# Five table stores of a two-block transformer kernel, issued from GpSimd's queue instead of SyncE's

## The chip, the cores and the metric

The kernel runs on one core of one Trainium2 chip. The metric is the device time of one execution in microseconds (us), lower is better. A core has five engines with an instruction queue each: TensorE (PE, matrix products), VectorE (DVE), ScalarE (ACT), GpSimd (POOL) and SyncE (SP, which here only issues DMA transfers). Any of SP, ACT and POOL can issue a DMA; the transfers themselves run on 16 DMA engines.

## The reference

Two transformer blocks run one after the other on a sequence of T = 512 rows of width D = 1024, all in float32. The first block mixes with an mLSTM and a stick-breaking attention and ends with an MLP; the second is a sparse attention with three branches (compressed, selected, window), each with a relative position bias. The two places that matter here:

```python
def first_block(...):
    ...
    x = x + y.astype(x.dtype) @ w_out[l]
    h2 = rms_norm(x, norm_mlp_g[l])
    x = x + jnp.square(jax.nn.relu(h2 @ w_up[l])) @ w_down[l]      # the MLP, d_ff = 4096
    return x

def nsa_compressed(q, kc, vc, table):                              # second block
    ...
    bias = table[t5_bucket(dist)].astype(jnp.float32)              # table: 32 buckets x 16 heads
    p = masked_softmax(logits + bias, dist >= 0)
```

The bias depends on the distance and the head alone, so it can be made long before the attention that uses it.

## The kernel before, in words

**Weights.** All weight matrices lie in DRAM as a list of tiles of 128 x 1024 float32 (512 KB), in the order of use. The class Weights walks through it. For each tile, SP loads it into a buffer wr (L169; three buffers), ACT casts it to a rounded high part wh (L172; four buffers), and DVE or POOL takes the difference as a low part wl (L174; four buffers). A product is then three matmuls: high x high, high x low, low x high (L341 to L343 in `gen_t`, L374 to L376 in `gen_n`).

**The MLP** (`mlp`, L740) runs in two halves f. In each, 16 steps m = 0 to 15 make 128 hidden columns each: `proj_t` does 24 matmuls with one weight tile into one PSUM bank b, and then ACT reads the bank with Relu (L761), squares (L763) and rounds it (hh, L305), and DVE takes the low part hl. Then `proj_n` multiplies by the second matrix. The eight PSUM banks are used in a ring.

**The tables.** In half 0, ahead of step m = 6, `bias_tables` makes two tables for the second block. The first, tr, has 16 rows (one a head) of 384 floats. It is stored to the DRAM tensor bt_d, repeated 128 times for each head, in four DMAs of 16 x 32 x 384 floats (768 KB each). The second, cb, is the compressed branch's table, stored to cb_d in one DMA of 128 x 2048 floats (1024 KB). The second block reads bt_d at L1256 and cb_d at L1031.

**What sets the order.** Each engine works through its own list in order, and the lists are fixed when the program is built. In the MLP a scheduler sets them from an estimate of its own of when things are ready; it is not the order of the Python lines. In the second block PE and POOL follow the written order. Before the change the five stores are handed to SP one at a time, ahead of steps m = 7 to 11 (`stores.pop(0)()`, L757).

Of the kernel before, what the change touches and what calls it, by code (L numbers as in the profile page):

```python
# [253 lines left out]
def tile_blocks(ctx, tc, x, xt, wts, prm, cst, table, post_g, w2k, w2v, out):  # L254
    nc = tc.nc
    v, s, g, pe, sy = nc.vector, nc.scalar, nc.gpsimd, nc.tensor, nc.sync
# [6 lines left out]
    def ring(*ids):  # L263
        turn = [0]

        def take():
            i = ids[turn[0] % len(ids)]
            turn[0] += 1
            return banks.tile([128, T], F32, name=f"b{i}", tag=f"b{i}", bufs=1)
        return take  # L270
# [17 lines left out]
    def small(shape, name, bufs=2):  # L288
        return glob.tile(shape, F32, name=name, tag=name, bufs=bufs)

    def ts(out_, in_, s1, s2=None, op0=OP.mult, op1=None, eng=None):
        if s2 is None:
            (eng or v).tensor_scalar(out_, in_, s1, None, op0)
        else:
            (eng or v).tensor_scalar(out_, in_, s1, s2, op0, op1)  # L295

    def stt(out_, a, sc, b, op0, op1):
        v.scalar_tensor_tensor(out_, a, sc, b, op0, op1)  # L298

    def tt(out_, a, b, op=OP.mult, eng=None):  # L300
        (eng or v).tensor_tensor(out_, a, b, op)  # L301

    def hi_lo(hi, lo, src, hi_in=None, scale=None):
        if scale is None:
            s.copy(hi, src)  # L305
            tt(lo, src, hi.bitcast(F32), OP.subtract)
        else:
            s.activation(hi, src, AF.Identity, scale=scale)
            stt(lo, src, scale, hi.bitcast(F32), OP.mult, OP.subtract)
# [39 lines left out]
    def proj_t(psum, acts, w=None, m=128):  # L349
        got = []  # L350
        emit(gen_t(psum, acts, got.append, w, m))
        return got[0]
# [28 lines left out]
    def proj_n(psum, acts, tail=1):  # L381
        got = {}
        emit(gen_n(psum, acts, got.__setitem__, tail))
        return [got[tb] for tb in range(4)]

    def transposed_acts(psum, src, gain):
        acts = []
        for kt in range(KT):
            ps = psum()
            for tb in range(4):  # L390
                pe.transpose(ps[:, 128 * tb:128 * tb + 128], src[:, tb, 128 * kt:128 * kt + 128], ident)
            h, l = act_tiles(kt)
            hi_lo(h, l, ps, scale=col(gain, kt))
            acts.append((h, l))
        return acts
# [294 lines left out]
    bt_d = dram.tile([16, 128, 384], F32, name="bt_d")  # L690
    x2_d = dram.tile([128, 4, D], F32, name="x2_d")
    cb_d = dram.tile([128, 4, 16, 32], F32, name="cb_d")

    def bias_loads(pb):
        tb_ = pb.tile([32, 16], F32, name="tb_")
        sy.dma_start(tb_, table)
        t31 = pb.tile([32, 16], F32, name="t31")
        sy.dma_start(t31, table[31:32, :].to_broadcast([32, 16]))
        oh = pb.tile([32, 384], F32, name="oh")
        sy.dma_start(oh, cst[0:32, C_OH:C_OH + 384])  # L700
        mr = pb.tile([16, 384], F32, name="mr")
        sy.dma_start(mr, cst[0:16, C_MASKR:C_MASKR + 384])
        ohc = pb.tile([128, 512], F32, name="ohc")
        sy.dma_start(ohc, cst[:, C_OHC:C_OHC + 512])
        mc = pb.tile([128, 16], F32, name="mc")
        sy.dma_start(mc, cst[:, C_MASKC:C_MASKC + 16])
        tt(tb_, t31, tb_, OP.subtract)
        bd = pb.tile([128, 4, 16], F32, name="bd")
        v.memset(bd, 0.0)
        for i in range(4):  # L710
            v.tensor_copy(bd[32 * i:32 * i + 32, i, :], tb_)
        return tb_, oh, mr, ohc, mc, bd

    def bias_tables(psum, pb, tb_, oh, mr, ohc, mc, bd):
        ps = psum()
        pe.matmul(ps[0:16, 0:384], tb_, oh, start=True, stop=True)
        tr = pb.tile([16, 384], F32, name="tr")
        tt(tr, ps[0:16, 0:384], mr, OP.add)
        ps = psum()
        for i in range(4):  # L720
            pe.matmul(ps[:, 64 * i:64 * i + 64], ohc[:, 128 * i:128 * i + 128],
                      bd.rearrange("p a b -> p (a b)"), start=True, stop=True)
        near = pb.tile([128, 16, 16], F32, name="near")
        tt(near, ps[:, 0:256].rearrange("p (k h) -> p h k", h=16),
           mc[:, None, :].to_broadcast([128, 16, 16]), OP.add)
        cb = pb.tile([128, 4, 16, 32], F32, name="cb")
        v.memset(cb, -NEG)
        for tb in range(4):
            lo, hi = max(0, 8 * tb - 9), 8 * tb + 7
            if lo > 0:  # L730
                v.memset(cb[:, tb, :, 0:lo], 0.0)
            k0 = lo - 8 * tb + 9
            v.tensor_copy(cb[:, tb, :, lo:hi], near[:, :, k0:k0 + hi - lo])
        stores = [(lambda i: lambda: sy.dma_start(bt_d[:, 32 * i:32 * i + 32, :],
                                                  tr[:, None, :].to_broadcast([16, 32, 384])))(i) for i in range(4)]
        stores.append(lambda: sy.dma_start(cb_d, cb))
        return stores

    def mlp(x1):
        with tc.tile_pool(name="ml", bufs=1) as ml, tc.tile_pool(name="pb", bufs=1) as pb:  # L740
            pj = ring(*range(8))
            acts = transposed_acts(pj, x1, P_GMLP)
            tables = bias_loads(pb)
            ssq2 = small([128, 2, 4], "ssq2", 1)
            ssq = small([128, 4], "ssq")
            for tb in range(4):
                jk = glob.tile([128, D], F32, name="jk2", tag="wr", bufs=3)
                s.activation(jk, x1[:, tb, :], AF.Square, accum_out=ssq[:, tb:tb + 1])
            r2 = small([128, 4], "rs2")
            ts(r2, ssq, 1.0 / D, EPS, OP.mult, OP.add)  # L750
            v.reciprocal(r2, r2)
            for f in range(2):
                hid = []
                for m in range(16):
                    if f == 0 and m == 6:
                        stores = bias_tables(pj, pb, *tables)
                    if f == 0 and m > 6 and stores:  # L757
                        stores.pop(0)()
                    ps = proj_t(pj, acts)
                    a = ml.tile([128, T], F32, name="a", tag="ra", bufs=2)  # L760
                    s.activation(a, ps, AF.Relu)  # L761
                    a2 = ml.tile([128, T], F32, name="a2", tag="ra2", bufs=2)
                    s.activation(a2, a, AF.Square)  # L763
                    h = ml.tile([128, T], F32R, name="hh", tag="hh", bufs=18)
                    l = ml.tile([128, T], F32R, name="hl", tag="hl", bufs=18)
                    hi_lo(h, l, a2)
                    hid.append((h, l))
                for c in range(2):
                    ps = proj_n(pj, hid, 1 + 3 * f * c)
                    for tb in range(4):  # L770
                        xs = x1[:, tb, 512 * c:512 * c + 512]
                        stt(xs, ps[tb], r2[:, tb:tb + 1], xs, OP.mult, OP.add)
                        if f == 1:
                            sy.dma_start(x2_d[:, tb, 512 * c:512 * c + 512], xs)
                            jk = glob.tile([128, T], F32, name="jk4", tag="rb", bufs=1)
                            s.activation(jk, xs, AF.Square, accum_out=ssq2[:, c, tb:tb + 1])

        return ssq2
# [569 lines left out]

    xb = first_mixer()
    sums2 = mlp(xb)  # L1350
    with tc.manual_schedule(engines={mybir.EngineType.PE, mybir.EngineType.Pool}):
        nsa(xb, sums2)
# [55 lines left out]
```

## Time and profile before

| | |
|---|---|
| median of 3 runs | 1399.81 us (1399.77 to 1400.01) |
| the profiled execution | 1398.81 us |
| its span, first to last instruction | 1397.1 us |
| PE busy | 1337.3 us, 96% of the span |
| DVE, ACT, POOL busy | 58%, 47%, 19% of the span |
| mean granted TensorE clock | 0.990 of full speed |
| DMA, mean over the span | 90 GB/s |

The profile is of one execution. PE is busy nearly all the time, so what counts is where it is not, and where it runs at the lower clock. The times of the trace are us from the first instruction.

### The profile page before, as it was taken

What the parts mean: (1) busy time and instruction counts of PE and PEld (TensorE: products, weight loads), DVE (VectorE), ACT (ScalarE), POOL (GpSimd) and SP (SyncE); (2) the same over time, 40 slices, a digit from 0 to 9 for tenths busy, and PEclk for the clock granted to TensorE, in tenths of its full rate; (3) what the DMA queues carried; (4) which work ended last, traced back from release to release, by engine and by line L of the source; (5) the groups of instructions that cost most, each with busy time, mean ns of one, the idle gap of its engine ahead of it and who ended that gap; (6) DMA issues with size and microseconds to landing.
All of it is one profiled execution on the core that took longest, in us unless ns stands there. A gap on an engine that the chain in (4) does not pass through costs nothing.

```text
span 1397.1 us, 17790 instructions
## 1 busy us (share of the span) xinstructions
PE 1337.3 (96%) x6622; PEld 1090.3 (78%) x6622; DVE 808.5 (58%) x1596; ACT 650.6 (47%) x1273; POOL 261.2 (19%) x230
## 2 busy tenths in 40 slices
PE   9999999999999999989999999899788999999897
PEld 7977787778786888868888888788677878777776
DVE  4678535556667535232233323455988998988823
ACT  6577624443434325341135422254446656665522
POOL 0022101111101000000000000134536242333352
PEclk9999999999999999999999999999999999999999
DMA  7411121213131414843333323314223122121132
GB/s 232 137 46 47 61 91 61 91 49 103 46 106 46 154 57 142 110 166 92 100 94 93 104 91 121 125 50 130 75 71 106 54 61 61 53 68 46 55 121 76
DMA packets 42039, 125.31 MB, mean 90 GB/s; under 512 B 4528, under 2 KB 11232, under 8 KB 41696
## 3 DMA queue, kind: packets, MB, share of 16 engines
q1 hardware_dynamic: 41952, 124.17, 29.4%
q8 instruction: 52, 0.85, 0.2%
q14 instruction: 35, 0.29, 0.1%
HBM read 115.77 MB, written 8.39 MB: 89 GB/s over the span
## 4 chain that ended last, share of the span: by engine, by line
PE 59%; DVE 16%; issue 15%; ACT 6%; POOL 2%; DMA 1%; SPq 0%; POOLq 0%; DVEq 0%; ACTq 0%
PE b L375 9%; PE b L374 9%; PE b L376 9%; PE b L341 8%; PE b L343 8%; PE b L342 8%; DVE P L295 4%; DVE b L1176 2%; DVE ptall L301 2%; ACT wh L172 1%; PE b L827 1%; ACT P L1180 1%; PE b L1211 1%; PE b L544 1%; PE b L1195 1%
## 5 line engine op out<-in xcount | busy, mean ns | idle before, releaser
L172 ACT CAST wh<-wr 128x1024 fp32r<-128x1024 f32 (+3 forms) x204 | 207.6, 1020 | 385.9 <-PE b L376 222.7
L341 PE MATMUL b<-ah,wh 128*128 128x512 f32 x808 | 330.5, 409 | 6.3 <-ACT wh L172 5.9
L174 DVE TENSOR_TENSOR wl<-wr,wh 128x1024 fp32r<-128x1024 f32 (+2 forms) x142 | 169.2, 1194 | 281.1 <-ACT wh L172 280.7
L343 PE MATMUL b<-ah,wl 128*128 128x512 f32 x808 | 318.9, 395 | 0.6 <-DVE wl L174 0.5
L342 PE MATMUL b<-al,wh 128*128 128x512 f32 x808 | 318.2, 394 | 0.0
L343 PEld LDWEIGHTS b<-ah,wl 128*128 128x128 f32 x808 | 152.8, 189 | 35.4 <-DVE wl L174 1.8
L341 PEld LDWEIGHTS b<-ah,wh 128*128 128x128 f32 x808 | 153.0, 189 | 34.3 <-ACT wh L172 6.7
L174 POOL TENSOR_TENSOR wl<-wr,wh 128x1024 fp32r<-128x1024 f32 (+1 forms) x62 | 143.6, 2320 | 159.0 <-ACT wh L172 149.4
L342 PEld LDWEIGHTS b<-al,wh 128*128 128x128 f32 x808 | 153.4, 190 | 24.5 <-issue 0.5
L374 PE MATMUL b<-wh,ah 128*128 128x512 f32 (+3 forms) x352 | 125.9, 359 | 1.0 <-ACT wh L172 0.6
L376 PE MATMUL b<-wh,al 128*128 128x512 f32 (+3 forms) x352 | 125.5, 357 | 0.1
L375 PE MATMUL b<-wl,ah 128*128 128x512 f32 (+3 forms) x352 | 125.3, 356 | 0.1
L1180 ACT ACTIVATE P<-b,nm 128x128 f32<-128x128 f32 (+3 forms) x128 | 67.5, 528 | 104.8 <-DVE nm L1176 102.6
L375 PE MATMUL b<-wl,hh 128*128 128x512 f32 x256 | 102.1, 399 | 0.0
L374 PE MATMUL b<-wh,hh 128*128 128x512 f32 x256 | 100.9, 394 | 0.0
L376 PE MATMUL b<-wh,hl 128*128 128x512 f32 x256 | 100.4, 392 | 0.0
L295 DVE TENSOR_SCALAR P<-P,rd,gn 128x128 f32<-128x128 f32 (+3 forms) x128 | 93.4, 730 | 2.5
L301 POOL TENSOR_TENSOR rsr<-rsm,mhalf 128x2 f32<-128x2 f32 (+1 forms) x3 | 2.4, 802 | 476.6 <-DVE rsm L295 476.6
L374 PEld LDWEIGHTS b<-wh,ah 128*128 128x128 f32 x352 | 66.2, 188 | 9.8 <-ACT wh L172 0.9
L376 PEld LDWEIGHTS b<-wh,al 128*128 128x128 f32 x352 | 66.4, 189 | 8.8 <-DVE al L298 0.5
L375 PEld LDWEIGHTS b<-wl,ah 128*128 128x128 f32 x352 | 66.4, 189 | 8.4 <-DVE wl L174 0.5
L1195 PE MATMUL b<-ident,P 128*128 128x128 f32 x320 | 56.7, 275 | 12.7 <-DVE ptall L301 10.4
(286 smaller groups left out, 2213.5 us busy)
## 6 DMA issues: line engine op xcount, KB each, us to landing
wr<-in_wts_dram SPq DMA_DIRECT2D x188, 512.0 KB, 3.5
bt_d<-tr SPq DMA_DIRECT2D x4, 768.0 KB, 20.5
wr<-in_wts_dram SPq DMA_DIRECT2D x8, 280.0 KB, 2.6
xk<-in_xt_dram SPq DMA_DIRECT2D x8, 256.0 KB, 3.8
xn<-in_x_dram SPq DMA_DIRECT2D x4, 512.0 KB, 4.9
xbig<-in_x_dram SPq DMA_DIRECT2D x1, 2048.0 KB, 9.9
x_d<-xbig SPq DMA_DIRECT2D x8, 256.0 KB, 2.9
bt<-bt_d SPq DMA_DIRECT2D x8, 256.0 KB, 2.7
```

Of the source, the lines that this page charges most:

```text
L172: nc.scalar.copy(hi, raw)
L174: eng.tensor_tensor(lo, raw, hi.bitcast(F32), OP.subtract)
L295: (eng or v).tensor_scalar(out_, in_, s1, s2, op0, op1)
L301: (eng or v).tensor_tensor(out_, a, b, op)
L341: pe.matmul(o, a, ah, start=(kt == 0), stop=False)
L342: pe.matmul(o, a, al, start=False, stop=False)
L343: pe.matmul(o, b, ah, start=False, stop=(kt == KT - 1))
L374: pe.matmul(o, ah[:, tsl], a, start=(kk == 0 and k == 0), stop=False)
L375: pe.matmul(o, ah[:, tsl], b, start=False, stop=False)
L376: W.last = pe.matmul(o, al[:, tsl], a, start=False, stop=end)
L1180: latest[0] = s.activation(P[:, 0:n], S[:, 0:n], AF.Exp, bias=nm, scale=-1.0, accum_out=rd)
L1195: pe.transpose(pst[:, 128 * sb:128 * sb + 128], P[:, 128 * sb:128 * sb + 128], ident)
```

## The change

`bias_tables` no longer returns a list of stores for `mlp` to hand out; it issues all five itself, at its end, on POOL's queue (`g` is GpSimd, `sy` is SyncE). What is stored, and where to, is the same.

```diff
-        stores = [(lambda i: lambda: sy.dma_start(bt_d[:, 32 * i:32 * i + 32, :],
-                                                  tr[:, None, :].to_broadcast([16, 32, 384])))(i) for i in range(4)]
-        stores.append(lambda: sy.dma_start(cb_d, cb))
-        return stores
+        for i in range(4):
+            g.dma_start(bt_d[:, 32 * i:32 * i + 32, :], tr[:, None, :].to_broadcast([16, 32, 384]))
+        g.dma_start(cb_d, cb)
...
                 for m in range(16):
                     if f == 0 and m == 6:
-                        stores = bias_tables(pj, pb, *tables)
-                    if f == 0 and m > 6 and stores:
-                        stores.pop(0)()
+                        bias_tables(pj, pb, *tables)
                     ps = proj_t(pj, acts)
```

The lists of instructions change in three places. On SP, in half 0 of the MLP, the stores stood between loads of weight tiles (wr); the difference of the two lists there is:

```order
-L169 DMA wr<-in_wts_dram 128x1024 x9
-L734 DMA bt_d<-tr 16x32x384 x3
-L169 DMA wr<-in_wts_dram 128x1024
-L734 DMA bt_d<-tr 16x32x384
-L169 DMA wr<-in_wts_dram 128x1024
-L736 DMA cb_d<-cb 128x2048
-L169 DMA wr<-in_wts_dram 128x1024 x48
+L169 DMA wr<-in_wts_dram 128x1024 x59
```

The five stores are gone and the loads stand in one row of 59. On POOL they now stand together between the last instruction of the first mixer (L626) and the first of the second block (the second L301 here, a power of -1/2):

```order
 L626 AFFINE_SELECT be<-be 128x128
+L735 DMA bt_d<-tr 16x32x384 x4
+L736 DMA cb_d<-cb 128x2048
 L301 TENSOR_TENSOR rsr<-rsm,mhalf 128x2
```

On ACT, though no line of the diff is about it, the scheduler has put four casts of weight tiles elsewhere. Before, this stood there from the end of step m = 10 to the Relu of step m = 13 (b_5017, b_5056 and b_5095 are the PSUM banks of steps 11, 12 and 13; wh<-wr is the cast of a weight tile for a later step):

```order
L305 CAST hh<-a_5004 128x512
L761 ACTIVATE a<-b_5017 128x512
L763 ACTIVATE a_5044<-a 128x512
L305 CAST hh<-a_5044 128x512
L172 CAST wh<-wr 128x1024
L761 ACTIVATE a<-b_5056 128x512
L763 ACTIVATE a_5083<-a 128x512
L305 CAST hh<-a_5083 128x512
L172 CAST wh<-wr 128x1024 x4
L761 ACTIVATE a<-b_5095 128x512
```

And now, for the same steps:

```order
L305 CAST hh<-a_5005 128x512
L172 CAST wh<-wr 128x1024
L758 ACTIVATE a<-b_5017 128x512
L760 ACTIVATE a_5044<-a 128x512
L305 CAST hh<-a_5044 128x512
L172 CAST wh<-wr 128x1024
L758 ACTIVATE a<-b_5056 128x512
L760 ACTIVATE a_5083<-a 128x512
L305 CAST hh<-a_5083 128x512
L172 CAST wh<-wr 128x1024
L758 ACTIVATE a<-b_5095 128x512
```

Before, no cast stands between the banks of steps 7 and 11; one follows step 11 and four follow step 12. Now one cast stands behind every step. DVE's differences wl move with them in the same way against its hl. Apart from this, the lists of PE, DVE, ACT and POOL hold the same instructions in the same order as before, down to the end of the program.

## Rows read from the trace of the kernel before

**Rows 1.** The page: span, TensorE's busy time, the chain that ended last

```profile
span 1397.1 us, 17790 instructions
...
PE 1337.3 (96%) x6622; PEld 1090.3 (78%) x6622; DVE 808.5 (58%) x1596; ACT 650.6 (47%) x1273; POOL 261.2 (19%) x230
...
PE 59%; DVE 16%; issue 15%; ACT 6%; POOL 2%; DMA 1%; SPq 0%; POOLq 0%; DVEq 0%; ACTq 0%
```

**Rows 2.** Waits, 540 to 640 us: who waited for whom, total us, times, longest

```profile
PE b L341 <- ACT wh L172: 5.9, 2, 2.9
...
ACT wh L172 <- DMA wr<-in_wts_dram: 3.2, 1, 3.2
```

**Rows 3.** PE's timeline in half 0: start us, us, instruction, idle before and releaser

```profile
561.18 0.48 PE L341 MATMUL b<-ah,wh 128*128 128x512 f32 x1
...
593.73 0.39 PE L343 MATMUL b<-ah,wl 128*128 128x512 f32 x1
597.06 0.50 PE L341 MATMUL b<-ah,wh 128*128 128x512 f32 x1 [2.94 <-ACT wh L172]
...
604.56 0.39 PE L343 MATMUL b<-ah,wl 128*128 128x512 f32 x1
607.89 0.73 PE L341 MATMUL b<-ah,wh 128*128 128x512 f32 x1 [2.94 <-ACT wh L172]
...
620.74 0.39 PE L341 MATMUL b<-ah,wh 128*128 128x512 f32 x1
...
626.19 0.39 PE L374 MATMUL b<-wh,hh 128*128 128x512 f32 x1
```

**Rows 4.** ACT's timeline in half 0, columns as in the rows of PE

```profile
559.41 1.04 ACT L172 CAST wh<-wr 128x1024 fp32r<-128x1024 f32 x1 [2.58 <-PE b L342]
...
572.17 1.05 ACT L172 CAST wh<-wr 128x1024 fp32r<-128x1024 f32 x1 [2.58 <-PE b L342]
...
577.84 0.60 ACT L761 ACTIVATE a<-b 128x512 f32<-128x512 f32 x1 [2.81 <-PE b L343]
...
594.15 0.60 ACT L761 ACTIVATE a<-b 128x512 f32<-128x512 f32 x1 [3.53 <-PE b L343]
...
595.97 1.04 ACT L172 CAST wh<-wr 128x1024 fp32r<-128x1024 f32 x1
...
606.79 2.94 ACT L172 CAST wh<-wr 128x1024 fp32r<-128x1024 f32 x3
```

**Rows 5.** Windows of 4 us: length, busy by engine, granted clock, DMA share, GB/s

```profile
556.00:560.00 4.00, 4.00 (x18) 2.73 (x17) 0.97 (x2) 1.39 (x3) 0.00 (x0) 1.00 0.42 135
...
564.00:568.00 4.00, 4.00 (x19) 3.30 (x19) 0.48 (x3) 1.27 (x2) 0.00 (x0) 1.00 0.92 99
...
596.00:600.00 4.00, 2.41 (x6) 1.69 (x7) 1.92 (x2) 1.01 (x2) 0.00 (x0) 0.72 0.90 349
...
604.00:608.00 4.00, 1.05 (x6) 0.56 (x5) 0.82 (x2) 2.96 (x5) 0.00 (x0) 1.00 0.00 0
608.00:612.00 4.00, 3.90 (x10) 2.62 (x11) 3.36 (x3) 1.73 (x2) 0.00 (x0) 0.58 0.43 120
```

**Rows 6.** SP's queue in time: start us, us of issuing, transfers

```profile
560.95 5.10 SPq L734 DMA_DIRECT2D bt_d<-tr  x3
566.17 4.42 SPq L169 DMA_DIRECT2D wr<-in_wts_dram  x1
...
898.84 0.62 SPq L1031 DMA_DIRECT2D Pc<-cb_d  x1
```

**Rows 7.** DMA issues of the whole span: count, KB each, median us to landing

```profile
bt_d<-tr SPq DMA_DIRECT2D x4, 768.0 KB, 20.5
...
cb_d<-cb SPq DMA_DIRECT2D x1, 1024.0 KB, 19.4
```

**Rows 8.** The tile wr, 530 to 640 us: its 19 loads, us to landing

```profile
DMA to landing us min/median/max: 3.3/3.6/21.4
```

**Rows 9.** POOL's timeline around the place of the stores

```profile
883.52 0.69 POOL L301 TENSOR_TENSOR rsr<-rsm,mhalf 128x2 f32<-128x2 f32 x1 [448.67 <-DVE rsm L295]
```

## The prediction

> **What bounds the kernel now.** I read the page first: PE is busy for 1337.3 of 1397.1 us, and the chain that ended last runs mostly over PE [rows 1]. Work that is taken off another engine is therefore worth nothing by itself; the change can only pay where PE stands still or runs at its lower clock. So the second view was the list of waits around the five stores. It has PE waiting twice for a cast of a weight tile, 2.9 us each time, and ACT waiting once for a weight transfer, 3.2 us [rows 2].
>
> Third, PE's timeline gives the price of this stretch. Step m = 6 starts at 561.18, and `proj_n`, which follows step 15, at 626.19 [rows 3]: 65.01 us for ten steps. An undisturbed step, the last of them, takes 626.19 - 620.74 = 5.45 us, so ten should take 54.5. The stretch loses **10.5 us**. Step 11's last matmul starts at 593.73 and, at 0.23 us a matmul (5.45 / 24), is through at 593.96; step 12 starts at 597.06. Step 12 in turn is through at about 604.8 and step 13 starts at 607.89; both gaps are put down to the cast wh [rows 3]. The idle time is 2 x 2.94 = 5.9 us of the 10.5; the rest is the clock, which after the gaps is granted at 0.72 and 0.58 over 4 us where it was 1.00 before them [rows 5], so part of each window runs at 1.2 instead of 2.4 GHz.
>
> Fourth, why the cast is late. Up to step 8 ACT casts one tile a step, as soon as PE gives a buffer free (559.41, 572.17) [rows 4]. Then comes a run of Relu groups with no cast, from 577.84 to the one at 594.15, and the next cast is at 595.97, behind step 11's own Relu group [rows 4]. ACT's list puts it there. Step 12 needs this cast, so PE can't start before ACT has read what PE has just made: the gap is built into the order. It is the same at 606.79, where three casts run in a row behind step 12's group [rows 4]. In that window, 604 to 608 us, the DMA share is 0.00 [rows 5]: no transfer was under way, so the second gap is the order's and not a transfer's. (At the first gap the engines are 0.90 busy [rows 5], so there the trace alone does not separate the two.)
>
> **The change part by part.**
>
> *SP loses five stores.* Three of them hold SP for 5.10 us from 560.95, and the load behind them, step 12's tile, is issued at 566.17 over 4.42 us [rows 6]. PE waits for none of this directly: price 0. But that load can now be issued as soon as its wr buffer is free. There are four wh buffers, so the cast at 559.41, which waits for step 5's last use of one [rows 4], is for step 9; its wr buffer is free once DVE has taken the difference behind it, at about 563 (an estimate: the cast ends at 560.45, and DVE has tr to make first). The load moves some 3 us earlier.
>
> *POOL gains five stores.* POOL's next instruction runs at 883.52 after 448.67 us of idle time [rows 9], and the tables are first read at 898.84 [rows 6]. From 561 on that leaves 322 us. Neither POOL's time to make the transfers nor their landing is on the path unless the whole takes fifteen times the 20.5 us that one store took [rows 7]. Price 0; without that cover it would push the second block's start.
>
> *ACT's and DVE's lists.* One cast stands behind every step, so step 12's tile can be cast at about 577 to 578, when step 8 frees its buffer, instead of 595.97. If its data is there, both gaps go, and with them the time at the lower clock: **minus 10.5 us**. PE's list is the same, and so is everything behind the MLP; the waits of the later stages are between PE, ACT and DVE and don't know at what time they start, so I let the 10.5 us through to the end.
>
> *The transfers themselves.* The same bytes go over the same 16 engines, so this is where the gain could be lost. The stores alone run at 0.92 busy and 99 GB/s [rows 5], and four of 0.786 MB take 3.15 MB / 0.099 = 31.8 us, 29.2 us of busy engines. The weight loads in 556 to 560 move 135 GB/s at a share of 0.42, so 321 GB/s when busy [rows 5]: 1.6 us for a tile of 0.524 MB, every 5.45 us, or 30% of the engines. At that rate cb's 1.05 MB [rows 7] take 3.3 us. Stores are then 32.5 us of work. If the loads get the 30% that they ask for, the stores are done about 32.5 / 0.7 = 46 us after 561, at 607, and no load is short. Before, SP's queue was shared: a load behind stores took up to 21.4 us to land instead of 3.6 [rows 8]. No row shows two queues side by side. Lower bound for a load: 3.6 us. Upper bound: it gets nothing until all stores are through, at 561 + 32.5 = 593.5, and lands at about 597. I take turn and turn about, a load of 4 to 10 us, because a load is asked for 14 us ahead of its cast (three buffers wr, 5.45 us a step, less the difference) and the cast stands another three steps ahead of its use: even 21.4 us would leave PE running.
>
> The Trainium skill, "DMA: Bandwidth & Descriptors", section "Queues, rings and completion order", says that each DMA engine goes round the queues that have work, a packet at a time; by it the loads get their turns, as in the sum. No run here shows it so far.
>
> *A new queue in use.* The execution is 1.7 us longer than its span (1398.81 against 1397.1 [rows 1]). I know of no row for what a first transfer from POOL adds there or at the end; between 0 and another 1.7 us, and I take 0.
>
> *Sum.* 1398.81 - 10.5 = 1388.3 for the profiled execution. That one is 1.0 under the median of the runs, 1399.81, so the median should be **1389.3 us**.
>
> **The rivals.** A difference of 0.2%, 2.8 us, is about what a measurement of this kernel can tell from none.
>
> *B, the loads come last.* POOL's stores are all queued within a short time, and if the engines favour them, step 12's tile lands at the upper bound, 597. The cast adds 1.04 us, so PE stands from 593.96 to 598: 4 us, and some 2 us of lower clock (before, 2.94 us of idle time cost 5.2 in all). Step 13 follows without a gap, since its tile lands 1.6 us later and has a cast of its own. Gain 10.5 - 6 = 4.5: 1395.3 us. For it: the share of 0.92 shows that the stores alone can fill the engines. Against it: nothing in the trace favours one queue.
>
> *C, nothing changes.* The stores are not removed, only issued elsewhere, and the engines stay as full. The Trainium skill, in the same page's section "Issuing engines are not separate DMA queues", says that the issuing engine changes only the sequencer's issue time, usually small beside the transfer. Taken alone, the trace's form of it is that SP's issue time is off the path, price 0, and the time stays at 1399.8 us. Against it stands the DMA share of 0.00 in the second gap: there PE waited for ACT's order, and that does change. What would still give 1399.8 is a first load so late that one stall costs as much as the two, PE starting step 12 at 593.96 + 10.5 = 604.5.
>
> *D, slower: transfers issued by POOL are less efficient.* If the same stores kept the engines busy twice as long and went first, they would be through at 561 + 65 = 626, step 12's tile at about 630 and its cast at 631. PE would stand 37 us: 1399.8 - 10.5 + 37 = 1426 us. It turns into a loss when step 12's cast ends behind 604.5, that is when the stores take over 1.2 times as long and the loads get no turn. For it: no row shows a transfer issued from POOL. Against it: sizes and shapes of the pieces are the same as now, and both conditions must hold.
>
> **How the numbers follow.** Forecast 0.78, B 0.08, C 0.07, D 0.07. The order of the lists is certain and the second gap is clearly its work; what is open is the transfers. The forecast's own range is 1388.3 to 1392 (the new queue's cost; a short first stall). Together with B it holds 0.86, so the range is 1387.5 to 1396.5. Forecast and B are faster by over 0.2%, C is the same, D is slower: 0.86, 0.07, 0.07.
>
> **What would show each step.** Right: between the start of step 6 and the first L374 matmul of `proj_n` some 54.7 us instead of 65.01; no wait of PE for wh there; granted clock 1.00 in every window; ACT's cast of step 12's tile near 577; wr landing well under 21.4 us while a POOL queue stores; POOL's instruction behind the stores waiting for DVE as before. Wrong: a wait of ACT's cast for wr that lasts beyond 594 (B, C, D by its length); loads that land after the stores only; stores that take longer than 46 us (D); the stretch shorter, but the second block longer by as much.

## The result and the profile after

| | before | changed |
|---|---|---|
| median | 1399.79 us, 4 runs (1398.02 to 1400.01) | 1386.97 us, 4 runs (1386.83 to 1387.41) |
| ratio of the runs | | 0.9912 (0.9895 to 0.9929) |
| the profiled execution, its span | 1398.81, 1397.1 us | 1387.11, 1385.2 us |

The kernel is 12.8 us faster. That is on the forecast's side and 2.3 us more than its 1389.3 us, half a microsecond below the lower end of the range.

The page of the changed kernel, its first lines, the DMA queues (packets, MB, share of the engines' time) and the stores' issues:

```profile
span 1385.2 us, 17815 instructions
...
PE 1331.9 (96%) x6622; PEld 1087.3 (78%) x6622; DVE 809.2 (58%) x1596; ACT 650.8 (47%) x1273; POOL 264.5 (19%) x235
...
q1 hardware_dynamic: 39696, 119.98, 27.3%
q0 software_dynamic: 912, 4.19, 2.3%
...
bt_d<-tr POOLq DMA_DIRECT2D x4, 768.0 KB, 21.9
```

The 4.19 MB of stores have moved from q1, SP's, to a new queue q0. The stretch that the prediction priced is the first to compare. PE's timeline from step 6 to the first matmul of `proj_n`, now without a gap:

```profile
561.05 0.48 PE L341 MATMUL b<-ah,wh 128*128 128x512 f32 x1
...
615.36 0.40 PE L343 MATMUL b<-ah,wl 128*128 128x512 f32 x1
615.59 0.39 PE L374 MATMUL b<-wh,hh 128*128 128x512 f32 x1
```

54.54 us, against 65.01 [rows 3]: 10.47 us less, the sum's 10.5. In the list of waits from 556 to 620 us no matmul of PE waits for a cast any more; this is what stands there of ACT's casts, with the waits' total, times and longest:

```profile
DVE wl L174 <- ACT wh L172: 32.7, 11, 10.2
ACT wh L172 <- DMA wr<-in_wts_dram: 19.4, 4, 9.8
ACT wh L172 <- PE b L342: 11.1, 4, 4.5
```

So the loads are late, four times, and ACT waits for them where PE doesn't. ACT's timeline has the four casts, steps 12 to 15, in order (start, duration in us, idle before and releaser):

```profile
584.73 1.05 ACT L172 CAST wh<-wr 128x1024 fp32r<-128x1024 f32 x1 [9.83 <-DMA wr<-in_wts_dram]
...
590.83 1.05 ACT L172 CAST wh<-wr 128x1024 fp32r<-128x1024 f32 x1 [3.24 <-DMA wr<-in_wts_dram]
...
599.01 1.05 ACT L172 CAST wh<-wr 128x1024 fp32r<-128x1024 f32 x1 [5.32 <-DMA wr<-in_wts_dram]
...
602.91 1.06 ACT L172 CAST wh<-wr 128x1024 fp32r<-128x1024 f32 x1 [1.03 <-DMA wr<-in_wts_dram]
```

At 5.45 us a step from 561.05, step 12 begins at 593.8, step 14 at 604.7. Step 12's cast is through 8 us before its step and step 14's 4.6 us: the tiles that were cast ahead were used up to a part, but not wholly. The tile wr, its six loads issued from 562 to 605 us (durations of the issue in ns, first and last start):

```profile
L169 SPq DMA_DIRECT2D wr<-in_wts_dram x6: 327/328/328, 562.9 to 601.4; - x6
...
DMA to landing us min/median/max: 4.3/18.8/24.6
```

POOL's timeline shows what its part costs: 2.75 us for four stores, and what comes next waits for DVE as before [rows 9]:

```profile
561.46 2.75 POOL L735 DMA_DIRECT2D bt_d<-tr  x4 [126.79 <-ACT a L758]
564.61 0.59 POOL L736 DMA_DIRECT2D cb_d<-cb  x1 [0.40 <-DVE cb L733]
872.93 0.71 POOL L301 TENSOR_TENSOR rsr<-rsm,mhalf 128x2 f32<-128x2 f32 x1 [307.73 <-DVE rsm L295]
```

**Where the rest of the gain is.** PE reaches `proj_n` 10.60 us earlier (626.19 against 615.59). The second block's transposes of its second half of rows (16 matmuls of 128 x 128) are a later mark. Before:

```profile
907.23 1.91 PE L813 MATMUL b<-ident,xbig 128*128 128x128 f32 x16
```

and after, with PE's wait that stands ahead of it:

```profile
888.86 0.39 PE L824 MATMUL b<-al,wh 128*128 128x256 f32 x1 [3.07 <-DVE al L298]
...
895.71 1.91 PE L810 MATMUL b<-ident,xbig 128*128 128x128 f32 x16
```

The lead is 11.52 us there, 0.92 more. At the end of the span it is 11.9, and 11.70 for the profiled executions. What is left to the 12.8 of the medians, 1.1 us, is that before's profiled execution was 1.0 us under its median and the changed kernel's 0.14 over its own.

### The profile page after: what moved, and what is told of

It is laid out like the page before. It is cut to its first block, busy times and chain, and to the rows that moved or that the text cites. A ratio compares the mean times of both kernels' runs of the same rounds, so it can differ in the third digit from the quotient of the medians.

```text
span 1385.2 us, 17815 instructions
## 1 busy us (share of the span) xinstructions
PE 1331.9 (96%) x6622; PEld 1087.3 (78%) x6622; DVE 809.2 (58%) x1596; ACT 650.8 (47%) x1273; POOL 264.5 (19%) x235
## 3 DMA queue, kind: packets, MB, share of 16 engines
q0 software_dynamic: 912, 4.19, 2.3%
## 4 chain that ended last, share of the span: by engine, by line
PE 60%; issue 15%; DVE 15%; ACT 5%; POOL 3%; DMA 1%; SPq 0%; POOLq 0%; DVEq 0%; ACTq 0%
PE b L375 9%; PE b L374 9%; PE b L376 9%; PE b L341 8%; PE b L342 8%; PE b L343 8%; DVE P L295 3%; DVE b L1173 2%; DVE ptall L301 2%; ACT wh L172 1%; PE b L824 1%; ACT P L1177 1%; PE b L1208 1%; PE b L544 1%; PE b L1192 1%
## 5 line engine op out<-in xcount | busy, mean ns | idle before, releaser
L301 POOL TENSOR_TENSOR rsr<-rsm,mhalf 128x2 f32<-128x2 f32 (+1 forms) x3 | 2.4, 806 | 334.6 <-DVE rsm L295 334.6
```

## The experiments

All ratios are to the kernel before, timed on the same chip in the same job. Its medians there were 1398.79 us (23 runs, 1397.34 to 1403.71), 1398.71 and 1398.96 us.

**1. ACT's order without the queue.** The stores stay with SP. ACT's list alone is written by hand for steps 7 to 15:

```diff
+                    if f == 0 and m == 7:
+                        by_hand = tc.manual_schedule(engines={mybir.EngineType.Activation})
+                        by_hand.__enter__()
                     ps = proj_t(pj, acts)
...
+                    if f == 0 and m == 15:
+                        by_hand.__exit__(None, None, None)
```

> The stores stay in SP's queue as before; ACT's list is fixed by hand in steps 7 to 15, so that a cast stands behind every step, one step later than in the changed kernel. Order theory (PE waited because ACT's casts stood behind PE's own results): both gaps go, the stretch is 54.6 to 57 us, and the time is 1386 to 1389 us, as with the change. Queue theory (the loads were late because they stood behind the stores in SP's queue): step 12's tile still lands at about 587 and the later ones at 595 to 600, PE waits for casts that wait for loads, and the time stays at 1395 to 1400 us.

Measured: 1387.90 us, ratio 0.9912 (0.9900 to 0.9925), the same as the change. PE has no wait in the stretch, which takes 54.54 us from its two rows:

```profile
563.99 0.48 PE L341 MATMUL b<-ah,wh 128*128 128x512 f32 x1
...
618.53 0.39 PE L374 MATMUL b<-wh,hh 128*128 128x512 f32 x1
```

The loads are as late as in the changed kernel, and land in time all the same. Its wr loads of 561 to 605 us:

```profile
DMA to landing us min/median/max: 5.1/16.8/21.4
```

**2. The queue without ACT's order.** The stores go to POOL as in the change. Loads are issued as ever, but the casts of steps 12 to 15 are held back, and ACT's list in steps 7 to 15 is written by hand, so that it reads as before the change but for one earlier cast, which comes a step later:

```diff
+                    if f == 0 and m == 9:
+                        W.hold = True
                     ps = proj_t(pj, acts)
...
+                    if f == 0 and m == 11:
+                        W.cast(1)
+                    if f == 0 and m == 12:
+                        W.cast()
+                        W.hold = False
```

> The stores go to POOL's queue as in the change, and ACT's list is held by hand to what it was before: no cast between the banks of steps 8 and 11, one behind step 11, four behind step 12. Order theory: both gaps are back, 2.9 us each and the lower clock behind them, and the time is 1397 to 1400 us, as before the change. Queue theory: the loads no longer stand behind the stores, so the time is 1387 to 1390 us.

Measured: 1397.59 us, ratio 0.9998 (0.9988 to 1.0008): with the queue changed and the order not, nothing is won. PE's timeline has both gaps back, as [rows 3] has them:

```profile
596.79 0.50 PE L351 MATMUL b<-ah,wh 128*128 128x512 f32 x1 [2.94 <-ACT wh L183]
...
607.88 0.50 PE L351 MATMUL b<-ah,wh 128*128 128x512 f32 x1 [2.94 <-ACT wh L183]
```

Experiments 1 and 2 together settle the cause: ACT's order is enough, and the queue alone is worth nothing here.

**3. Both kernels again.** No edit, five rounds each, for their spread and a second trace.

(The lengths of 3.4 and 6.8 us that expectations name are those of the stretches at the lower clock in the traces.)

> The kernel before, unchanged, for its spread and a second trace. Two readings of what the prediction left out (the time fell by 12.8 us, the stretch of half 0 accounts for 10.5). Clock reading: after each stall PE runs for a while at the lower clock, and how long differs from execution to execution, so the runs of this kernel, which has two stalls more, spread over 1 to 3 us, and in its trace the stretch from step 6 to proj_n again costs 65 us or some us more (65 to 69), with the time at the lower clock as the difference. Second-block reading: the stretch is 65.0 again to 0.1 us, and the entry of the second block takes the same time as in the first trace.

> The changed kernel, unchanged. Clock reading: 1386.5 to 1388.5 us, ratio 0.990 to 0.9925; the stretch from step 6 to proj_n is 54.6 us with no wait of PE, and the entry of the second block varies by up to 2 us from the first trace of it. Second-block reading: the entry is as in the first trace of the changed kernel, 0.9 us shorter than before, to 0.1 us.

Measured: 1397.76 us (11 runs, 1396.95 to 1404.00; ratio 0.9995, 0.9983 to 1.0007) and 1385.76 us (4 runs, 1385.67 to 1388.43; ratio 0.9910, 0.9897 to 0.9923). Two of the expected numbers were missed: before's runs spread over 7 us and not 1 to 3, and the changed kernel's median is 0.7 us under the lowest expected. In the second trace of the kernel before, step 6 and `proj_n` start at

```profile
560.38 0.48 PE L341 MATMUL b<-ah,wh 128*128 128x512 f32 x1
...
627.12 0.39 PE L374 MATMUL b<-wh,hh 128*128 128x512 f32 x1
```

66.74 us, where the first trace had 65.01. The idle time is the same, 2.94 us twice and 0.5 us once for DVE. The granted clock is not; the second trace's windows (length, busy by engine, clock, DMA share, GB/s):

```profile
596.00:600.00 4.00, 3.71 (x8) 2.50 (x9) 1.23 (x1) 0.20 (x1) 0.00 (x0) 0.50 0.79 291
600.00:604.00 4.00, 4.00 (x14) 3.10 (x13) 0.00 (x0) 0.00 (x0) 0.00 (x0) 0.65 0.11 45
...
608.00:612.00 4.00, 3.23 (x8) 2.32 (x9) 3.50 (x3) 2.09 (x3) 0.00 (x0) 0.71 0.36 97
612.00:616.00 4.00, 4.00 (x16) 3.18 (x16) 1.23 (x1) 1.05 (x1) 0.00 (x0) 0.87 0.83 296
```

After the first gap the clock is now at the lower level (1.2 GHz) through one window and most of another, 0.50 and 0.65. The first trace had 0.72 [rows 5] and then

```profile
600.00:604.00 4.00, 4.00 (x16) 3.19 (x16) 0.00 (x0) 0.00 (x0) 0.00 (x0) 0.86 0.21 81
```

The same two gaps of 2.94 us cost 1.7 us more. The changed kernel's stretch is 54.54 us in its first trace and 54.55 in its second (561.77 to 616.32). At the entry of the second block PE's wait for DVE is 3.07 us in the first trace of the changed kernel and 3.01 in the second, but the clock behind it differs. First trace:

```profile
890.00:894.00 4.00, 4.00 (x23) 4.00 (x23) 2.00 (x5) 1.39 (x4) 0.00 (x0) 0.59 0.76 225
894.00:898.00 4.00, 4.00 (x37) 4.00 (x36) 1.14 (x3) 1.65 (x5) 0.00 (x0) 1.00 0.00 0
```

and second:

```profile
890.00:894.00 4.00, 4.00 (x20) 4.00 (x20) 2.71 (x6) 2.09 (x5) 0.00 (x0) 0.50 0.87 268
894.00:898.00 4.00, 4.00 (x31) 4.00 (x31) 0.00 (x0) 0.00 (x1) 0.00 (x0) 0.86 0.07 23
```

From the first matmul of `proj_n` to the transposes named above it is 281.04 and 279.85 us in the two traces of the kernel before, and 280.12, 281.04 and 281.04 in the three of the changed kernel (the third is that of experiment 6). So the 0.92 us at the entry does not belong to the change: either kernel shows both the longer and the shorter time. Nor is the price of the two gaps a constant of the kernel before. The second-block reading falls.

**4. Twice the stores.** Every store is made a second time to DRAM that nobody reads, from POOL in the changed kernel, and from SP in the kernel of experiment 1:

```diff
+        for i in range(4):
+            g.dma_start(bt_e[:, 32 * i:32 * i + 32, :], tr[:, None, :].to_broadcast([16, 32, 384]))
+        g.dma_start(cb_e, cb)
```

> The changed kernel with every store made a second time from POOL's queue, to DRAM that nobody reads (8.4 MB in place of 4.2). In the trace of the change the loads get nothing for some 12 us after the stores begin and then turns, one packet for one, that give a load in 5.5 to 7.3 us where a step needs 5.45. Turns reading: the 3 us of slack left at step 14 run out, PE falls behind by 1.5 us a tile until the stores end at about 650, and the time is 1391 to 1402 us. If the loads get all that they ask for: no wait of PE, 1385 to 1389 us.

> The kernel with stores in SP's queue and a cast behind every step, with every store made a second time from SP's queue. Step 12's tile stands behind 43 us of stores and lands at about 606, step 13's at 622, step 14's at 635. Queue-matters-when-full reading: PE stands about 15 us at step 12 and 30 to 35 in all, time 1415 to 1428 us, much worse than the same bytes from POOL's queue. If the queue is worth nothing at all: as the doubled stores from POOL.

Measured: 1392.59 us from POOL, ratio 0.9958 (0.9945 to 0.9972), and 1421.14 us from SP, ratio 1.0160 (1.0147 to 1.0174); both times within what was expected. The waits came otherwise. With POOL, PE was expected to fall behind from step 14 on; its ten steps still take 54.54 us, and its first wait is at 624.56, in `proj_n`:

```profile
624.56 0.50 PE L374 MATMUL b<-wh,hh 128*128 128x512 f32 x1 [2.72 <-ACT wh L172]
```

and with SP, from step 12 on:

```profile
609.85 0.79 PE L341 MATMUL b<-ah,wh 128*128 128x512 f32 x1 [13.57 <-ACT wh L172]
...
625.97 0.80 PE L341 MATMUL b<-ah,wh 128*128 128x512 f32 x1 [7.69 <-ACT wh L172]
...
637.59 0.50 PE L341 MATMUL b<-ah,wh 128*128 128x512 f32 x1 [2.75 <-ACT wh L172]
```

With SP the waits sum to 24.0 us, where 30 to 35 were expected; with the time at the lower clock the ten steps take 87.66 us, 33.1 more than without waits. SP's queue shows what makes its loads later than POOL's stores do:

```profile
563.11 9.63 SPq L736 DMA_DIRECT2D bt_d<-tr  x4
...
581.72 4.48 SPq L169 DMA_DIRECT2D wr<-in_wts_dram  x1
```

The six stores ahead of step 12's load hold SP for 18.4 us. That load is issued at 581.72 and takes 27.0 us to land; with the stores in POOL's queue it is issued at 563.4 and takes 21.2, and two more loads are issued before it lands. With 8.4 MB the queue is worth 28.5 us; with 4.2 MB it was worth nothing, because the tiles ahead covered either lateness.

**5. ACT's queue.** The five stores from ACT, by `s.dma_start` in place of `g.dma_start`.

> The changed kernel with the five stores issued from ACT's queue. A queue of its own is enough: loads get turns, and the casts stand behind every step, so the time is 1385 to 1390 us although ACT is held for some 14 us while it issues (SP's later stores took 4.4 us each). If ACT's time in issuing counts, its Relu groups and casts are late by more than the three cast tiles ahead (16 us), PE waits, and the time is 1392 to 1400 us.

Measured: 1386.92 us, ratio 0.9916 (0.9903 to 0.9930). ACT is held by issuing, as these rows of its timeline show (ACTq is its queue), and PE doesn't wait. But the loads did not get the turns that were expected. SP's queue, with a load issued at 562.5, has no packet up to 575, and in 582 to 590 us, with three loads under way, only ACT's queue moves anything (534 packets, 92.2% of the engines' time). Step 13's cast waits 12.0 us for its load and ends at 597.5, 1.4 us before its step begins: it was the tiles held ahead that kept PE running.

```profile
561.53 8.49 ACTq L735 DMA_DIRECT2D bt_d<-tr  x2
570.07 4.47 ACTq L736 DMA_DIRECT2D cb_d<-cb  x1
574.58 0.60 ACT L758 ACTIVATE a<-b 128x512 f32<-128x512 f32 x1 [12.43 <-issue]
```

**6. Filling the wait at the entry of the second block.** 24 matmuls into a spare PSUM bank, behind the first half of the entry's products; then, as the trace showed them behind the wait, 32 ahead of it:

```diff
+                if kt == 0:
+                    spare = av()
+                    for _ in range(32):
+                        pe.matmul(spare[:, 0:256], first[0][1][0][:, 0:128], acts[0][0][:, 0:256],
+                                  start=True, stop=True)
```

> The changed kernel with 24 matmuls of 128x256 into a bank that nobody reads, put on PE where it waits 3.1 us at the entry of the second block. Clock reading: PE no longer stands still, the stretch at the lower clock (3.4 us in one trace of the changed kernel, 6.8 in the other) goes, and the time falls by 1.7 to 3.4 us against the changed kernel, to 1382 to 1385 us, with less spread. If the stretch at the lower clock costs nothing there, since the next waits are DVE's and ACT's: no change.

> The changed kernel, unchanged, as the partner of the next run: 1385.5 to 1388 us, with PE's wait of 3.0 to 3.1 us for DVE at the entry of the second block and 3.4 or 6.8 us at the lower clock behind it.

> The changed kernel with 32 matmuls of 128x256 into a bank that nobody reads, this time ahead of PE's wait at the entry of the second block (the first attempt put its 24 behind it, where they only cost their 3.0 us). At 0.12 us each they take 3.8 us, as long as the two waits together. Clock reading: no stretch at the lower clock near 889, 1.7 to 3.4 us less than the changed kernel beside it, 1382.5 to 1385.5 us. If what waits behind is DVE's and ACT's: the lower clock goes but the time stays within 1 us.

Measured: the first, misplaced one 1390.70 us, ratio 0.9945 (0.9932 to 0.9959). It tells nothing of the clock; its 24 matmuls ran behind the wait and were only work on the path:

```profile
901.51 3.04 PE L1303 MATMUL b<-ah,wh 128*128 128x256 f32 x24
```

The second, beside the changed kernel on the same chip: 1384.79 us, ratio 0.9898 (0.9880 to 0.9917), against 1387.10 us, ratio 0.9912 (0.9895 to 0.9928). The intervals overlap, so the 2.3 us between the two are not clear of noise by themselves; of the runs, 3 of its 4 lie under all 5 of the changed kernel's (1384.30 to 1385.05, the fourth 1386.49; 1386.14 to 1389.25). Its windows at the entry have the full clock:

```profile
886.00:890.00 4.00, 3.98 (x33) 3.78 (x32) 3.55 (x6) 1.26 (x4) 0.77 (x1) 1.00 0.74 235
890.00:894.00 4.00, 4.00 (x36) 4.00 (x35) 1.36 (x3) 1.12 (x4) 0.00 (x0) 1.00 0.62 175
```

The changed kernel beside it, in its own windows of the same place:

```profile
890.00:894.00 4.00, 3.85 (x18) 3.86 (x19) 2.91 (x8) 2.16 (x5) 0.00 (x0) 0.50 0.86 245
894.00:898.00 4.00, 4.00 (x29) 4.00 (x29) 0.38 (x1) 0.00 (x0) 0.00 (x0) 0.79 0.18 61
```

From `proj_n` to the transposes it takes 278.68 us with the 32 matmuls, against 281.04 in the changed kernel beside it. That kernel has the lowest median of all that was run.

## Why the prediction was right in its direction and a little short

*The mechanism* was right. The gaps stood in ACT's order and went with it (experiments 1 and 2), in the place and, in that trace, to 0.1 us of the size that was read from it. The granted clock is 1.00 in every window of the stretch, as foreseen. Why the scheduler moved the casts when the stores left SP's list is not shown.

*The size* was 2.3 us short. The step that failed is the last of the part on ACT's and DVE's lists: "minus 10.5 us", the price of the gaps in one execution, was let "through to the end" as the whole gain, and the sum then carried it over to the medians, with a range that reached only 1.8 us below it. The gain measured is 11.70 us between the profiled executions and 12.8 between the medians. Of the 2.3 us, 0.92 came at the entry of the second block, where a wait of 3 us is followed by a longer or shorter time at the lower clock in the same kernel (experiment 3): the luck of the two traces. Another 1.1 is the distance of the two profiled executions from their medians, which the prediction took to be the same for both kernels; 0.3 is spread over the rest.

The price of the gaps is itself no constant: 65.01 - 54.54 = 10.5 us in the trace at hand and 66.74 - 54.54 = 12.2 in the second, by the time at the lower clock alone; in experiment 2, which has both gaps back, the stretch is 65.35 us and the price 10.8. The kernel before spreads over 6.4 us in 23 runs: the six with a mean granted clock of 0.985 to 0.987 took 1398.95 to 1403.71 us, the other 17, at 0.989 to 0.991, 1397.34 to 1399.72. The later two comparisons of both kernels give 13.0 and 11.9 us between the medians, so 10.5 was too little each time. That the clock accounts for the medians' distance too is argued from two traces of before and three of after (in which the stretch is 54.54, 54.55 and 54.54 us), not shown run by run. A forecast from one trace should have gone some 2 us further down at its lower end.

*The transfers* went otherwise than I took them to, without effect. I took 4 to 10 us for a load, and under 21.4 as a sign of being right; the measured median is 18.8 and the longest 24.6. The queues' shares show why. The DMA queues in 564 to 574 us, in the changed kernel:

```profile
q0 software_dynamic: 231, 0.97, 98.1%
```

and in 576 to 596 us:

```profile
q0 software_dynamic: 451, 1.87, 82.5%
q1 hardware_dynamic: 414, 1.54, 18.8%
```

For ten microseconds the load that SP had issued at 562.9 got no packet at all (q1 is not in the first list); then the two queues took turns, 451 packets against 414. Turns by the packet are what the Trainium skill, "DMA: Bandwidth & Descriptors", section "Queues, rings and completion order", states; these counts agree with it, and the ten microseconds before them do not show it. And a turn is not a fair share of time: the stores hold the engines for 82.5% against 18.8%. By these rows a packet of the stores takes an engine about four times as long as one of the loads (an estimate, 16 engines x 20 us x share / packets: 0.59 us against 0.15), though its bytes are nearly the same (4.1 KB against 3.7). What was decisive was the other number of that part, that a tile is asked for 14 us and three steps ahead of its use, some 30 us, and it bore the lateness. The cast of step 12 was foreseen near 577 and came at 584.73, for the same reason.

*POOL's part* was right: 2.75 us of issuing, and the instruction behind it waited for DVE. *A new queue in use*, bounded at 0 to 1.7 us, cost nothing that shows: what lies around the span is 1.9 us (1387.11 less 1385.2) against 1.7.

*The rivals.* B needed loads that come last and PE waiting for them; loads came late, and PE did not wait. C was right for the queue taken alone, which the forecast also priced at 0: experiment 2 is that case, and its time is that of before to 0.1%. What C left out is ACT's order. The rule beside it, in the Trainium skill's same page, section "Issuing engines are not separate DMA queues", agrees with experiment 2. Its "usually small" does not hold in experiment 4, where the six stores hold SP for 18.4 us ahead of a load that PE comes to wait for, and the queue is worth 28.5 us. D needed POOL's transfers to be less efficient. The pieces were not cut the same, as it assumed (912 packets against 2256, below), but the stores took 2.3% of the engines' time from POOL's queue and 2.2% from ACT's (experiment 5); the last landed at 602.7 (issued at 564.61, 38.1 us to landing), where the sum had 607.

## What to carry to other kernels

When a scheduler orders the engines' lists, compare the lists before pricing a change of queue: here the diff named five DMAs, and the gain lay in four casts on ACT that the diff doesn't mention. Ask of a wait whether the awaited instruction was late because its input was, or because of what stands ahead of it in its own list; a window in which no transfer is under way answers it. And price a gap on TensorE as its idle time plus a time at the lower clock that is different in each execution, so take a range for it from more than one trace, or leave room for it below as well as above.

## What was not expected of the hardware

With stores queued from POOL, a load of another queue first got no packet for 10 us, and only then took turns with them. With the stores in ACT's queue it got none for 12 us, and again none for 8 us later on, so this is not special to POOL's queue. What causes it was not tried and stays open. The two kinds of queue also cut the same stores into different packets: the 4.19 MB are 912 packets from POOL's queue and, from ACT's in experiment 5, 2256.

```profile
q10 hardware_dynamic: 2256, 4.19, 2.2%
```

Issuing cost POOL 0.6 to 0.9 us a store, and held ACT and SP 4.1 to 4.6 us for most of theirs (the rows of ACT above; [rows 6] for a load behind stores). Whether a full queue is what held them is not shown.
